# Modulation sums of an encoder layer: more of their terms on VectorE, one sum over partitions by matmul

## The chip, the cores and the metric

The kernel runs on one core of a Trainium2 chip. The metric is the device time of one execution in microseconds; the time before is the median of three runs. The core has a TensorE (PE in the profile; PEld is its weight load), a VectorE (DVE), a ScalarE (ACT), a GpSimd (POOL) and a SyncE (SP), which issues most of the plain loads. Each engine works its own list of instructions in order; the engines meet through semaphores.

## The reference

One layer of a streaming encoder on 1024 tokens of width 1024, in float32. Six vectors of 1024 numbers, made from one conditioning vector, shift, scale and gate the layer:

```python
cond = jax.nn.silu(c)
for l in range(DEPTH):                                   # DEPTH = 1
    mod = (cond @ w_mod[l] + b_mod[l])[:, None, :]       # w_mod: 1024 x 6144
    sh1, sc1, gt1, sh2, sc2, gt2 = jnp.split(mod, N_MOD, axis=-1)
    h = rms_norm(x, g_mix[l]) * (1.0 + sc1) + sh1
    p = h @ w_in[l]
    ...                                                  # HGRN2, S5 and RG-LRU on column groups of p
    x = x + gt1 * (y @ w_out[l])
    h2 = rms_norm(x, g_ffn[l]) * (1.0 + sc2) + sh2
    x = x + gt2 * peer_ffn(h2, peer_w_q[l], peer_sub_keys[l], peer_u[l], peer_v[l])
return rms_norm(x, g_final)
```

`peer_ffn` scores 8 heads against two sets of 128 keys, takes the 16 best of 16384 experts per token and head, and sums the gated rows of two tables of 16384 x 1024. The change concerns `cond @ w_mod` alone: a sum over 1024 inputs, that is over 8 blocks of 128 (KT = 8), for 48 blocks of 128 columns.

## The kernel before

Tokens are worked in four fronts F0 to F3 of 256 tokens (two tiles of 128). A front (`front`, L345) normalizes its tiles (`norm_x` L326, `norm_T` with the transposes at L337 and their eviction at L340), projects them with w_in (TensorE, `bank<-hT,w`), runs the S5 and LRU scans (L402, L447 and others on VectorE), the HGRN levels (masks, products and matmuls in turn: L540, L558 to L562 on VectorE, `wq<-q,kk` on TensorE), and projects out (gt1 enters at L621, the residual at L622). Then come the product keys (`product_keys`, L642: scores `wq<-hT,w` and `wq<-skT,qT` on TensorE, top-16 searches at L684 to L688 and sorting at L733 to L736 on VectorE). Tiles 0, 1, 6 and 7 get their experts by gathered rows (POOL's indirect loads at L921 and L937, row sums at L927 and L942 on VectorE), which run from F1 on beside the fronts; tiles 2 to 5 get theirs from the dense phase, the last half of the span, in which TensorE goes through all experts in 128 groups (transposes at L842 first), fed by one-hot gates (L790 to L797).

The modulation is made in twelve groups of 512 columns by `mod_rows(a, nv)` (L192). A group loads its part of w_mod in four loads of 512 KB (`load_w2`, L187 to L189, issued by SP in order). They come from the pool `w` with WPB = 3 buffers, shared with w_in, w_q and w_out, so that a load can start only when the third load before it has been used up. Each load holds two of the eight terms. A term is summed in one of two ways: as a matmul with cond's column, broadcast over 128 columns, as the weight (L201, in the profile L139 of the helper `mm`), which adds the 128 inputs and leaves the result in all partitions; or on VectorE as w times cond's column, added to a running sum `sv` in SBUF (L204 for the first, L206 for the others). In the second case one matmul with the constant `ones` at the end (L208) adds the 128 partitions of `sv` into the same PSUM bank. `nv` is the number of terms of the second kind, `MV = (2, 0)` (L55): two for the first norm's groups (a = 0, 4, 8, 12; column-wise by `mod_cols`), none for the others.

The other eight groups lie in two places. `late_mod` (L293) makes gt1 (a = 16, 20, `bc_row`) and four groups for the second norm (a = 24 to 36, `mod_cols`); it is stepped by the HGRN levels of F0. `bc_row("gt2", 40)` (L985) makes the last two groups, a = 40 and 44, after F1's product keys; `bc_row` adds b_mod at L289.

The order on each engine is not that of the program text. A list scheduler simulates the engines and puts each instruction where its inputs and its place in the program let it come next; so the order of before and that of after differ beyond the changed lines.

Of the kernel before, what the change touches and what calls it, by code (L numbers as in the profile page):

```python
# [21 lines left out]
KT = DM // 128  # L22
# [29 lines left out]
UHB = 3  # L52
UB = 3
WPB = 3
MV = (2, 0)  # L55
GT2 = 1
PORD = 1
PSTEP = 2
# [29 lines left out]
def trunk(ctx, tc, x, c, w_mod, b_mod, g_mix, w_in, hgrn_lb_logits, s5_a_re, s5_a_im, s5_b_re, s5_b_im,  # L88
# [31 lines left out]
    def bank():  # L120
        return ps.tile([128, 512], F32, name="bank")
# [4 lines left out]
    def T2():  # L126
        return t2.tile([128, 512], F32, name="t2")
# [10 lines left out]
    def mm(o, l, r, st, sp):  # L138
        P_.matmul(o, l, r, start=st, stop=sp)  # L139
# [4 lines left out]
    ones = const.tile([128, 128], F32, name="ones")  # L144
# [42 lines left out]
    def load_w2(w, k0, c0):  # L187
        t = wp.tile([128, 2, 512], F32, name="w")
        D.dma_start(out=t, in_=w[k0 * 128:(k0 + 2) * 128, c0:c0 + 512].rearrange("(k p) n -> p k n", p=128))  # L189
        return t  # L190

    def mod_rows(a, nv):  # L192

        pm = bank()
        sv = None
        for k0 in range(0, KT, 2):
            w = load_w2(w_mod, k0, a * 128)
            for k in range(2):
                ck = cond[:, k0 + k:k0 + k + 1]
                if k0 + k < KT - nv:  # L200
                    mm(pm, ck.to_broadcast([128, 128]), w[:, k], k0 + k == 0, k0 + k == KT - 1)  # L201
                elif sv is None:
                    sv = T2()
                    V.tensor_scalar(sv, w[:, k], ck, None, op0=OP.mult)  # L204
                else:
                    V.scalar_tensor_tensor(sv, w[:, k], ck, sv, op0=OP.mult, op1=OP.add)  # L206
        if nv:
            mm(pm, ones, sv, False, True)  # L208
        return pm

    def mod_cols(a):
        pm = mod_rows(a, MV[0] if a < 16 else MV[1])
        for i in range(4):
            jk = TS()[:, 0:128]
            V.scalar_tensor_tensor(jk, pm[:, i * 128:i * 128 + 128], 1.0, ident, op0=OP.mult, op1=OP.mult,
                                   accum_out=mod[:, a + i:a + i + 1])
        V.tensor_tensor(mod[:, a:a + 4], mod[:, a:a + 4], cv("b_mod", a, 4), OP.add)
# [64 lines left out]
    def bc_row(nm, a):  # L282
        t = (keep if nm == "gt2" else const).tile([128, DM], F32, name=nm)
        for half in range(2):
            hs = slice(half * 512, half * 512 + 512)
            c0 = a * 128 + half * 512
            br = T2()
            D.dma_start(out=br, in_=b_mod[:, c0:c0 + 512].to_broadcast([128, 512]))
            V.tensor_tensor(t[:, hs], mod_rows(a + 4 * half, MV[1]), br, OP.add)  # L289
            yield  # L290
        bcast[nm] = t
# [1022 lines left out]
```

## Time and profile before

| | us |
|---|---|
| median of 3 runs | 3209.16 (3196.37 to 3212.6) |
| the profiled execution | 3212.96 |
| its span in the trace | 3211.1 |
| TensorE busy | 2838.5 (88%) |
| VectorE busy | 2663.5 (83%) |
| GpSimd busy | 1322.7 (41%) |

The span is what the profiler saw from the first instruction to the last; 1.86 us of the execution lie outside. A busy share over the whole span is a mean over stages that differ; the table of stretches among the rows below tells them apart. [...] A float32 matmul appears as two MATMUL instructions.

### The profile page before, as it was taken

The page shows a single profiled execution, that of the slowest core. Times are in us where ns is not written, and L with a number is a line of the kernel's source. Part 1 is how long each engine was busy: PE and PEld are TensorE (multiplying, and loading weights), DVE is VectorE, ACT ScalarE, POOL GpSimd, SP SyncE. Part 2 cuts the span into 40 slices and gives each one's busy share as a digit, 9 for nine tenths or more (in the row PEclk, how much of TensorE's full clock was granted, in tenths as well). Part 3 has the DMA queues.
Part 4 walks back from the last instruction along what each step waited for, and adds up shares of the span by engine and source line. Part 5 has one row for each costly group of instructions (what it writes and reads, how often), then busy time and mean ns, then how long its engine had stood idle before and what let it go on. Part 6 is the DMA issues. An engine that isn't in the chain of part 4 may idle for free.

```text
span 3211.1 us, 45551 instructions
## 1 busy us (share of the span) xinstructions
PE 2838.5 (88%) x16525; PEld 2424.6 (76%) x16525; DVE 2663.5 (83%) x5540; ACT 1043.6 (32%) x1993; POOL 1322.7 (41%) x1155
## 2 busy tenths in 40 slices
PE   5998976789788985779599999999999999999996
PEld 3765865476676865658588889889888998988896
DVE  6241798689987999879899989999989999899955
ACT  3312321133166560466622222222222222222222
POOL 0000156534454335541054545555655555355501
PEclk8998986799779995789699999999999999999998
DMA  5353597899689986886499999999999999999932
GB/s 156 110 164 125 169 309 237 311 349 314 209 286 345 302 293 219 284 322 228 145 325 339 349 328 346 344 342 344 348 341 323 343 345 347 313 333 335 351 118 77
DMA packets 490370, 896.73 MB, mean 279 GB/s; under 512 B 29609, under 2 KB 306721, under 8 KB 486049
## 3 DMA queue, kind: packets, MB, share of 16 engines
q0 software_dynamic: 147456, 536.94, 46.6%
q1 hardware_dynamic: 333312, 342.92, 32.8%
q10 hardware_dynamic: 9376, 13.96, 1.2%
q8 instruction: 131, 2.15, 0.3%
q14 instruction: 95, 0.77, 0.1%
HBM read 847.57 MB, written 46.14 MB: 278 GB/s over the span
## 4 chain that ended last, share of the span: by engine, by line
PE 14%; issue 12%; DMA 9%; POOL 8%; DVE 6%; ACT 1%; SPq 0%; POOLq 0%; ACTq 0%; DVEq 0%
PE A L139 7%; PE V L139 6%; DMA row<-in_peer_v_dram,eid 5%; POOL row L921 4%; POOL row L937 4%; DMA row<-in_peer_u_dram,eid 2%; DMA vn<-in_peer_v_dram 2%; DVE fin L942 2%; DVE row L927 1%; PE T L842 1%; DVE vl L869 1%; DVE acc L882 1%; DVE ul L844 1%; DVE ag L854 0%; DMA row<-x1d 0%
## 5 line engine op out<-in xcount | busy, mean ns | idle before, releaser
L937 POOL DMA_INDIRECT row<-in_peer_v_dram,eid x512 | 631.6, 1234 | 672.8 <-DVE fin L942 362.2
L921 POOL DMA_INDIRECT row<-in_peer_u_dram,eid x512 | 644.6, 1259 | 610.3 <-DVE row L927 308.0
L139 PE MATMUL V<-vh,w 128*128 128x256 f32 x4096 | 771.0, 283 | 8.6 <-ACT w L856 4.9
L942 DVE SCALAR_TENSOR_TENSOR fin<-row,wgt,fin 128x1024 f32<-128x1024 f32 x508 | 649.1, 1278 | 50.9 <-DMA row<-in_peer_v_dram,eid 48.6
L927 DVE SCALAR_TENSOR_TENSOR row<-row,h 128x1024 f32<-128x1024 f32 x512 | 619.3, 1219 | 85.5 <-DMA row<-in_peer_u_dram,eid 84.1
L139 PEld LDWEIGHTS V<-vh,w 128*128 128x128 f32 x4096 | 645.5, 189 | 19.3 <-ACT w L856 8.2
L139 PE MATMUL V<-vl,w 128*128 128x256 f32 x2048 | 563.1, 282 | 7.1 <-DVE vl L869 7.1
L139 PE MATMUL A<-hh,ul 128*128 128x512 f32 x1024 | 408.6, 399 | 19.6 <-DVE ul L844 19.4
L139 PE MATMUL A<-hh,uh 128*128 128x512 f32 x1024 | 414.0, 404 | 0.4 <-ACT uh L843 0.3
L139 PE MATMUL A<-hl,uh 128*128 128x512 f32 x1024 | 404.4, 395 | 0.0
L139 PEld LDWEIGHTS V<-vl,w 128*128 128x128 f32 x2048 | 388.3, 190 | 13.0 <-DVE vl L869 9.7
L867 ACT CAST vh<-vn 128x1024 fp32r<-128x1024 f32 x128 | 134.6, 1052 | 447.5 <-PE V L139 370.9
L139 PE MATMUL bank<-hT,w 128*128 128x256 f32 x1152 | 270.1, 392 | 9.9 <-DMA w<-in_w_in_dram 4.7
L139 PEld LDWEIGHTS bank<-hT,w 128*128 128x128 f32 x1152 | 222.3, 197 | 45.1 <-issue 6.3
L139 PE MATMUL wq<-hT,w 128*128 128x256 f32 x1024 | 239.6, 388 | 7.4 <-DMA w<-in_peer_w_q_dram 5.6
L139 PEld LDWEIGHTS A<-hh,ul 128*128 128x128 f32 x1024 | 194.1, 190 | 61.8 <-DVE ul L844 28.3
L139 PE MATMUL gk<-oh 128*128 128x128 f32 x1024 | 177.0, 328 | 62.0 <-ACT oh L794 45.6
L843 ACT CAST uh<-T 128x512 fp32r<-128x512 f32 x256 | 147.4, 586 | 258.7 <-PE T L842 250.1
L139 PEld LDWEIGHTS gk<-oh 128*128 128x128 f32 x1024 | 161.8, 229 | 82.0 <-ACT oh L794 55.0
L139 PEld LDWEIGHTS A<-hl,uh 128*128 128x128 f32 x1024 | 194.0, 189 | 36.5
L139 PEld LDWEIGHTS A<-hh,uh 128*128 128x128 f32 x1024 | 194.2, 190 | 34.6 <-ACT uh L843 1.1
L139 PEld LDWEIGHTS wq<-hT,w 128*128 128x128 f32 x1024 | 194.8, 196 | 33.7 <-issue 5.9
(419 smaller groups left out, 3999.8 us busy)
## 6 DMA issues: line engine op xcount, KB each, us to landing
vn<-in_peer_v_dram SPq DMA_DIRECT2D x128, 512.0 KB
un<-in_peer_u_dram SPq DMA_DIRECT2D x128, 512.0 KB
w<-in_w_in_dram SPq DMA_DIRECT2D x88, 512.0 KB
w<-in_peer_w_q_dram SPq DMA_DIRECT2D x64, 512.0 KB
gd<-stg SPq DMA_DIRECT2D x32, 1024.0 KB
gt<-gd SPq DMA_DIRECT2D x16, 2048.0 KB
w<-in_w_mod_dram SPq DMA_DIRECT2D x48, 512.0 KB
w<-in_w_out_dram SPq DMA_DIRECT2D x32, 512.0 KB
```

Of the source, the lines that this page charges most:

```text
L139: P_.matmul(o, l, r, start=st, stop=sp)
L842: P_.transpose(bk[:, k], un[:, kk * 128:kk * 128 + 128], ident)
L843: S.copy(uh, bk)
L844: V.tensor_tensor(ul, bk, uh.bitcast(F32), OP.subtract)
L867: S.copy(vh, vn)
L869: V.tensor_tensor(vl, vn, vh.bitcast(F32), OP.subtract)
L882: V.tensor_tensor(a, a, pv, OP.add)
L921: G.indirect_dma_start(out=ur, out_offset=None, in_=u_tab, in_offset=bass.IndirectOffsetOnAxis(ap=o.eid[:, k:k + 1], axis=0))
L927: V.scalar_tensor_tensor(ur, ur, 1.0, o.h2, op0=OP.mult, op1=OP.mult, accum_out=o.act[:, k:k + 1])
L937: G.indirect_dma_start(out=vr, out_offset=None, in_=v_tab, in_offset=bass.IndirectOffsetOnAxis(ap=o.eid[:, k:k + 1], axis=0))
L942: V.scalar_tensor_tensor(o.fin, vr, o.wgt[:, k:k + 1], o.fin, op0=OP.mult, op1=OP.add)
```

## The change

The first norm's groups now have four terms of eight on VectorE instead of two, and the eight other groups have all eight there instead of none. Where all eight are there, the ones-matmul is the only matmul of its group, and it starts the bank as well as closing it.

```diff
@@ -52,7 +52,7 @@
 UHB = 3
 UB = 3
 WPB = 3
-MV = (2, 0)
+MV = (4, 8)
 GT2 = 1
 PORD = 1
 PSTEP = 2
@@ -198,14 +198,14 @@
             for k in range(2):
                 ck = cond[:, k0 + k:k0 + k + 1]
                 if k0 + k < KT - nv:
-                    mm(pm, ck.to_broadcast([128, 128]), w[:, k], k0 + k == 0, k0 + k == KT - 1)
+                    mm(pm, ck.to_broadcast([128, 128]), w[:, k], k0 + k == 0, False)
                 elif sv is None:
                     sv = T2()
                     V.tensor_scalar(sv, w[:, k], ck, None, op0=OP.mult)
                 else:
                     V.scalar_tensor_tensor(sv, w[:, k], ck, sv, op0=OP.mult, op1=OP.add)
         if nv:
-            mm(pm, ones, sv, False, True)
+            mm(pm, ones, sv, nv == KT, True)
         return pm
 
     def mod_cols(a):
```

The scheduler's order moves with it. Three places are shown; in each row the line comes first, then the operation, the result and the inputs with their names, the shape, and how many such instructions stand in a row. On TensorE at gt2's place (`bank<-w,cond` are gt2's terms, `wq` F1's product keys, L337 the transposes of F2's normalized tiles `s_`, `bank<-hT,w` F2's projections), this stands before:

```order
L139 MATMUL wq<-skT,qT 128x128 x2
L139 MATMUL bank<-w,cond 128x512 x2
L139 MATMUL wq<-skT,qT 128x128 x2
L139 MATMUL bank<-w,cond 128x512 x8
L337 MATMUL bank<-ident,s_4649 128x128 x4
L139 MATMUL bank<-w,cond 128x512 x2
L337 MATMUL bank<-ident,s_4649 128x128 x4
L139 MATMUL bank<-w,cond 128x512 x2
L337 MATMUL bank<-ident,s_4677 128x128 x4
L139 MATMUL bank<-w,cond 128x512 x2
L337 MATMUL bank<-ident,s_4677 128x128 x4
L139 MATMUL bank<-hT,w 128x256 x72
```

Here gt2's matmuls and the transposes take turns. After the change, with `t_4623` and `t_4645` the two running sums that come from VectorE, the same place reads:

```order
L139 MATMUL wq<-skT,qT 128x128 x2
L139 MATMUL wq<-hT,w 128x256 x8
L139 MATMUL wq<-skT,qT 128x128 x4
L139 MATMUL bank<-t_4623,ones 128x512
L139 MATMUL bank<-t_4645,ones 128x512
L337 MATMUL bank<-ident,s_4665 128x128 x8
L337 MATMUL bank<-ident,s_4693 128x128 x8
L139 MATMUL bank<-hT,w 128x256 x72
```

F2's transposes stood among the last matmuls of gt2; now both ones-matmuls stand ahead of all of them.

On VectorE at the same place (L684 to L736 are F1's product keys, L942 the row sums of a gathered tile, L289 the addition of b_mod), this stands before:

```order
L942 SCALAR_TENSOR_TENSOR fin<-row,wgt,fin 128x1024
L733 TENSOR_TENSOR oh<-io_727,pf 128x800
L686 MATCH_REPLACE rest_4334<-vals,sc 128x128
L686 MATCH_REPLACE rest_4340<-vals,sc 128x128
L942 SCALAR_TENSOR_TENSOR fin<-row,wgt,fin 128x1024
L735 TENSOR_TENSOR oh<-oh,cidx 128x800
L719 CAST pf<-pos 128x64
L687 MAX vals<-rest_4334 128x8
L687 MAX vals<-rest_4340 128x8
L289 TENSOR_TENSOR gt_4605<-bank,t_4626 128x512
```

Here gt2 appears only as the addition at L289. After the change:

```order
L206 SCALAR_TENSOR_TENSOR t_4645<-w,cond,t_4645 128x512
L733 TENSOR_TENSOR oh<-io_727,pf 128x800
L942 SCALAR_TENSOR_TENSOR fin<-row,wgt,fin 128x1024
L688 MAX_INDEX inds<-vals,rest_4433 128x8
L704 TENSOR_TENSOR cand<-vals 128x4x16
L688 MAX_INDEX inds<-vals,rest_4439 128x8
L206 SCALAR_TENSOR_TENSOR t_4645<-w,cond,t_4645 128x512
L735 TENSOR_TENSOR oh<-oh,cidx 128x800
L942 SCALAR_TENSOR_TENSOR fin<-row,wgt,fin 128x1024
L695 CAST fi<-inds 128x128
L684 MAX best<-cand 128x8 x4
L736 TENSOR_REDUCE ef<-oh 128x2x8
```

The sixteen terms stand one by one between other operations, and the last of them stands just ahead of an L735 of F1's sorting. On VectorE in F0's HGRN levels (`q`, `kk` and `scT` are the levels' operands, `mod` the late columns), this stands before:

```order
L437 TENSOR_TENSOR u<-u,ys 128x512
L540 COPY_PREDICATED scT<-masks,wq 128x32x8 x2
L561 TENSOR_TENSOR q<-q,pr_1301 128x64x8
L562 TENSOR_TENSOR kk__759<-kk__759,pr_1301 128x64x8
L540 COPY_PREDICATED scT<-masks,wq 128x16x16 x2
L561 TENSOR_TENSOR q<-q,pr_1343 128x32x16
L562 TENSOR_TENSOR kk__759<-kk__759,pr_1343 128x32x16
L215 SCALAR_TENSOR_TENSOR s_1322,mod<-bank,ident 128x128
L215 SCALAR_TENSOR_TENSOR s_1324,mod<-bank,ident 128x128
L215 SCALAR_TENSOR_TENSOR s_1326,mod<-bank,ident 128x128
```

One level follows the other here. After the change:

```order
L540 COPY_PREDICATED scT<-masks,wq 128x32x8 x2
L561 TENSOR_TENSOR q<-q,pr_1309 128x64x8
L562 TENSOR_TENSOR kk__759<-kk__759,pr_1309 128x64x8
L289 TENSOR_TENSOR gt_1070<-bank,t_1116 128x512
L204 TENSOR_SCALAR t_1184<-w,cond 128x512
L206 SCALAR_TENSOR_TENSOR t_1184<-w,cond,t_1184 128x512 x7
L204 TENSOR_SCALAR t_1263<-w,cond 128x512
L206 SCALAR_TENSOR_TENSOR t_1263<-w,cond,t_1263 128x512 x7
L215 SCALAR_TENSOR_TENSOR s_1200,mod<-bank,ident 128x128
L215 SCALAR_TENSOR_TENSOR s_1202,mod<-bank,ident 128x128
L215 SCALAR_TENSOR_TENSOR s_1204,mod<-bank,ident 128x128
L204 TENSOR_SCALAR t_1316<-w,cond 128x512
```

Between two levels now stand the terms of two whole groups, one after the other.

## Rows read from the trace of the kernel before

**Rows 1.** The page's busy times, shares of the span and instructions of each engine.

```profile
PE 2838.5 (88%) x16525; PEld 2424.6 (76%) x16525; DVE 2663.5 (83%) x5540; ACT 1043.6 (32%) x1993; POOL 1322.7 (41%) x1155
```

**Rows 2.** Busy time by stretch of the span (start:end, length, engines, clock, DMA).

```profile
core 0: us, PE busy (x) PEld busy (x) DVE busy (x) ACT busy (x) POOL busy (x), PEclk, DMA share, GB/s
...
155.20:228.40 73.20, 71.80 (x375) 45.45 (x375) 34.34 (x88) 5.87 (x8) 0.00 (x0) 1.00 0.61 186
466.00:520.00 54.00, 31.82 (x190) 31.03 (x190) 52.66 (x93) 1.88 (x2) 32.64 (x23) 0.50 0.68 218
690.00:740.00 50.00, 45.43 (x202) 35.07 (x201) 50.00 (x249) 8.55 (x21) 17.71 (x28) 0.97 0.96 317
...
800.00:840.00 40.00, 29.38 (x169) 20.84 (x162) 40.00 (x86) 3.42 (x5) 15.46 (x14) 0.85 0.78 250
...
900.00:1040.00 140.00, 116.76 (x562) 93.98 (x563) 110.09 (x125) 91.22 (x219) 68.88 (x51) 0.87 0.93 331
1040.00:1220.00 180.00, 158.36 (x883) 134.97 (x881) 175.98 (x583) 95.99 (x213) 62.11 (x64) 0.93 0.87 292
...
1440.00:1600.00 160.00, 119.57 (x615) 105.73 (x614) 150.23 (x577) 105.75 (x248) 13.48 (x31) 0.81 0.54 187
1600.00:3200.00 1600.00, 1557.40 (x10227) 1403.15 (x10225) 1413.42 (x1882) 431.93 (x676) 797.04 (x642) 0.99 0.89 316
```

**Rows 3.** One term on each engine: nanoseconds (shortest/median/longest), first and last start.

```profile
L139 PE MATMUL bank<-w,cond x176: 592/592/1221, 12.9 to 747.2; 128*128 128x512 f32 x176
L204 DVE TENSOR_SCALAR t<-w,cond x4: 481/486/487, 22.7 to 51.4; 128x512 f32<-128x512 f32 x4
L206 DVE SCALAR_TENSOR_TENSOR t<-w,cond,t x4: 744/748/752, 23.8 to 52.0; 128x512 f32<-128x512 f32 x4
```

**Rows 4.** Instructions with cond alone, by place: PE, PEld, DVE, ACT.

```profile
12.00:54.00 42.00, 28.23 (x48) 10.92 (x48) 4.93 (x8) 0.21 (x1) 0.92 0.64 192
160.00:226.00 66.00, 44.29 (x96) 17.14 (x96) 0.00 (x0) 0.00 (x0) 1.00 0.62 190
724.00:750.00 26.00, 16.82 (x32) 6.18 (x32) 0.00 (x0) 0.00 (x0) 0.93 0.94 313
```

**Rows 5.** SP's timeline: start, length of the issuing, line, load, how many.

```profile
0.75 46.75 SPq L189 DMA_DIRECT2D w<-in_w_mod_dram  x16
...
151.37 67.05 SPq L189 DMA_DIRECT2D w<-in_w_mod_dram  x24
...
716.96 22.61 SPq L189 DMA_DIRECT2D w<-in_w_mod_dram  x8
741.48 50.08 SPq L184 DMA_DIRECT2D w<-in_w_in_dram  x14
```

**Rows 6.** TensorE's timeline at gt2 and the start of F2's projections.

```profile
732.06 7.11 PE L139 MATMUL bank<-w,cond 128*128 128x512 f32 x12 [3.00 <-DMA w<-in_w_mod_dram]
...
745.83 1.98 PE L139 MATMUL bank<-w,cond 128*128 128x512 f32 x4 [0.94 <-DMA w<-in_w_mod_dram]
...
749.84 17.53 PE L139 MATMUL bank<-hT,w 128*128 128x256 f32 x80 [1.59 <-ACT hT L340]
```

**Rows 7.** TensorE's timeline in F0: the last transposes and the first projection.

```profile
67.44 1.97 PE L337 MATMUL bank<-ident,s 128*128 128x128 f32 x8 [6.83 <-ACT s L329]
...
72.37 3.92 PE L139 MATMUL bank<-hT,w 128*128 128x256 f32 x15
```

**Rows 8.** VectorE's timeline: the L735 ahead of which the last term now stands.

```profile
775.37 0.98 DVE L735 TENSOR_TENSOR oh<-oh,cidx 128x800 f32<-128x800 f32 x1
```

**Rows 9.** TensorE's waits from 760 to 850: total, times, longest.

```profile
PE wq L139 <- DVE q L545: 6.8, 1, 6.8
PE wq L139 <- DVE kk__4705 L562: 6.2, 1, 6.2
PE wq L139 <- DVE kk__4705 L559: 3.8, 1, 3.8
```

## The prediction

> **What bounds the kernel now.** I read the shares of the engines first, then the same shares stage by stage, and then the two stages that the change touches, on the engines' own timelines. Over the whole span TensorE is busy 88% and VectorE 83% [rows 1], which decides nothing: the two take turns as the bound. The table by stretch shows it [rows 2]. From about 1600 us to the end (the dense experts) TensorE is busy 1557.40 of 1600 us, and nothing that the change touches lies there, so this stage moves as a block: what counts is when it starts. Ahead of it are the four fronts F0 to F3 and their routing. In 155.2 to 228.4, where F0's late modulation runs among the HGRN levels, TensorE has 71.80 of 73.20 us and VectorE only 34.34. From F1's end on it is the other way round: VectorE has 50.00 of 50 us in 690 to 740, 40.00 of 40 in 800 to 840, 175.98 of 180 in 1040 to 1220 and 150.23 of 160 in 1440 to 1600. Only 900 to 1040 leaves it much room, 110.09 of 140. So the change takes work from TensorE where TensorE is full, which is fair (the late modulation), and also where VectorE is full already (gt2, 717 to 750 us).
>
> The third thing to see is the pace of the weight loads. SP issues 16 loads for the first norm in 46.75 us, 24 for the late modulation in 67.05 us and 8 for gt2 in 22.61 us [rows 5]: 2.8 to 2.9 us for each load of two terms, three times the same. Two terms cost TensorE about 2.4 us (four instructions at 592 ns) and VectorE 1.5 us (two at 748 ns) [rows 3]. The loads, not the engine that takes them in, set the pace, so a cheaper consumer wins little by itself.
>
> **First norm's columns.** Two more of eight terms go to VectorE in each of four groups: 8 matmuls (16 of the 48 TensorE instructions there, 28.23 us in all [rows 4], so 9.4 us) against 8 VectorE operations of 748 ns [rows 3], 6.0 us. Both lie in a stretch paced by 16 loads. At best the end of the stage comes earlier by what the last group saves: its last two loads are drained by VectorE beside TensorE, and the ones-matmul comes after. Ends: 0 if the loads set it alone, and -6 if two thirds of the 9.4 us were on the path. I take -2, since the pace of 2.9 us is the same with and without VectorE's help.
>
> **Late modulation (six groups in F0).** Removed are 48 matmuls, 96 instructions and 44.29 us of TensorE [rows 4]; 6 ones-matmuls of two instructions return, 12 at 592 ns = 7.1 us. Added to VectorE are 6 groups of 0.486 + 7 x 0.748 = 5.72 us [rows 3], 34.3 us, on top of 34.34: 68.7 us of work in a stage that lasted 73.20 [rows 2]. The floor by VectorE is 68.7, by loads 67.05; so the most that can be won is 5. But VectorE's list is in order, and it holds two whole groups in a row between HGRN levels: 8 loads, at 2.8 us 22.4 us, against 11.4 us of terms, so VectorE stands some 11 us for loads there, with the levels' masks and products queued behind it, and TensorE waiting for those. 68.7 + 11 = 79.7, or +6. Ends: -5 (terms slip into gaps) and +16 (a second such wait). Most like the row of F1's levels (466 to 520), where VectorE has 52.66 of 54 us and TensorE gets no further for it. I take +6. With the first norm, +4.
>
> **gt2, the term that decides.** 16 matmuls, 32 instructions and 16.82 us of TensorE [rows 4] go; two ones-matmuls return. VectorE gets 2 x 5.72 = 11.4 us where it has no idle time [rows 2]. In the kernel before the last of these matmuls run at 732 to 747 us between F2's transposes, and F2's projections start at 749.84 [rows 6]. In the changed order both ones-matmuls stand ahead of F2's transposes on TensorE, and the sixteenth term stands on VectorE directly ahead of the L735 that started at 775.37 [rows 8]: the scheduler has spread the terms, one between every few steps of F1's product keys and row sums. TensorE, being in order, cannot begin F2 before that. Counting VectorE's list with the trace's durations, 8.3 of the 11.4 us stand ahead of that point net (3.1 us of other work moved behind it), so the last term ends near 783.7. Then a ones-matmul (1.1), the transposes and evictions: one tile took 4.93 us from the first transpose to its projection [rows 7], the second adds about 3. F2's projections start near 793, **+43** against 749.84. The w_in loads behind gt2's eight loads in SP's queue now wait for buffers that VectorE frees; the first w_in load needs only the buffer of the sixth load, so it lands well ahead of 793 and costs nothing beyond the +43 (if a row said otherwise, one load, 2.8).
>
> **What comes back.** While F2 is held, VectorE doesn't idle: the order moves some 42 us of other work (row sums and F1's routing) ahead of F2's first LRU operation. That work is then missing later, which shortens only stretches in which VectorE is the bound. In F2's own levels TensorE waited 6.8 + 6.2 + 3.8 = 16.8 us for VectorE [rows 9]; about 10 of it should go, as the routing that crowded VectorE is done. In 1040 to 1220 and 1440 to 1600, which are full [rows 2], the list is some 8 and 15 us shorter than before; I take half, 12. In 900 to 1040 VectorE has slack and nothing returns. The ends are 10 (only the levels) and 42 (all). I take 22, the middle, since the full and the slack stretches about share the time.
>
> Sum: 4 + 43 - 22 = **+25**. The profiled execution took 3212.96 us, 3211.1 of it the span; 3238. The median of the runs is 0.12% lower, so 3234.
>
> [...]
>
> **Rivals.** (1) The forecast: F2 is held behind VectorE's terms and about half comes back. For it speaks that both queues are in order and that VectorE is full there; 0.52. Its own range, from the ends above, is 3213 to 3256.
>
> (2) VectorE is the bound all the way from F1 to the dense phase: the whole 42 us comes back, and only the early +4 and a small rest, 5 to 13 us, remain: about 3218. For it speak the full stretches [rows 2]; against it the 30 us that VectorE idles in 900 to 1040, in which F2's chain and not VectorE's amount of work sets the end. 0.23.
>
> (3) Faster. The place is F2's stretch behind its projections, and the mechanism that VectorE's crowding was F2's real limit: then F2, started late, runs with an emptied VectorE and saves the 42 us of moved work and also the whole 16.8 us of its waits, while the early stages reach their floors (-2 and -5). 43 - 59 - 7 = -23, 3186 by the median. It decides from the point where more than 50 us are recovered. Against it: the moved row sums only lie on F2's chain where they stood between its operations, and F2's levels waited 16.8 us in all, not 50. 0.11.
>
> (4) Nothing comes back. TensorE, sparse in the late modulation and idle for some 45 us ahead of F2, falls to the lower clock, as in 466 to 520 [rows 2]; F2's first projections (17.53 us at full clock [rows 6]) take up to twice that, which eats the recovery, and the late stage is at its upper end, +16: -2 + 16 + 43 = +57, 3266 by the median. 0.14.
>
> That the change does nothing of the kind is out: TensorE's list holds 16 matmuls with the condition vector where it held 88.
>
> **How the numbers follow.** The time is that of (1), 3234. The range is 3206 to 3262: below it lies (3), above it half of (4) and a small tail of (1). About 0.5%, 16 us, is what a measurement of this kernel can tell from no change, so faster means below 3193 and slower above 3225. Faster: most of (3), 0.08. Same: (2), the rest of (3) and the lower part of (1), 0.31. Slower: the rest of (1) and (4), 0.61.
>
> **What would show it.** On TensorE's timeline of the changed kernel, F2's first projection near 793 (right), or near 750 (wrong: the hold isn't there). A gap on TensorE from about 728 to 784, ended by VectorE's sums. The late stage 74 to 84 us long instead of 73.2; under 70, and TensorE's relief was worth more than I gave it. The first matmuls of the dense phase some 25 us later than before: 45 or more speaks for (4), under 13 for (2), earlier for (3). In 900 to 1040 VectorE should still idle; if its idle time there is gone, (2) has taken the place of (1). The prediction is wrong in its main step if VectorE's last gt2 term ends before 765, because the terms did not have to wait for the work that stands ahead of them.

## The result and the profile after

The changed kernel takes 3242.11 us in the median of 6 runs (3231.94 to 3249.19), against 3210.55 us (3196.37 to 3213.58) for the kernel before: a ratio of 1.0111, interval 1.0092 to 1.0129. It is slower by some 32 to 36 us, and the interval lies clear of 1; 3234 with a range of 3206 to 3262 was forecast. The profiled execution took 3241.63 us with a span of 3239.8.

The busy times of the whole span, which answer to [rows 1], show that the work moved as planned and tell nothing of the loss: TensorE has 16397 instructions, 128 fewer, and is busy 2800.2 us, 38 less; VectorE has 5612, 72 more, and is busy 2712.2 us, 49 more.

Where it went is seen by following the same points of the program through both traces. The times are starts in us: the first projection of F0 and F2 on TensorE, the G projection at the end of F0's levels, the last residual (L622) of F2 and F3 and the first LRU operation (L447) of F3 on VectorE, the first transpose of the dense phase on TensorE.

| | before | after | later by |
|---|---|---|---|
| F0, first projection | 72.37 | 68.28 | -4.1 |
| F0, G projection | 244.64 | 245.78 | +1.1 |
| F2, first projection | 749.84 | 792.63 | **+42.8** |
| F2, last residual | 1006.3 | 1055.3 | +48.9 |
| F3, first LRU operation | 1119.1 | 1170.7 | +51.6 |
| F3, last residual | 1409.7 | 1443.6 | +33.9 |
| dense phase | 1595.88 | 1628.25 | +32.4 |
| end of the span | 3211.1 | 3239.8 | +28.7 |

Each start here and below comes from one profiled execution, and such starts scatter. In the nine kernels of this document that leave the first norm as it was, F0's first projection begins anywhere from 70.1 to 74.7. So a difference of 2 or 3 us says nothing, and one of 30 or 40 stands.

The step is at F2's start. TensorE's timeline there, which answers to [rows 6] (start, length, line, operation; in brackets the idle time before it and what ended it):

```profile
726.24 0.71 PE L139 MATMUL wq<-skT,qT 128*128 128x128 f32 x4 [0.84 <-ACT qT L656]
754.57 2.08 PE L139 MATMUL bank<-t,ones 128*128 128x512 f32 x2 [27.61 <-DVE t L206]
784.81 2.07 PE L139 MATMUL bank<-t,ones 128*128 128x512 f32 x2 [28.17 <-DVE t L206]
786.67 1.06 PE L337 MATMUL bank<-ident,s 128*128 128x128 f32 x4
...
792.63 13.44 PE L139 MATMUL bank<-hT,w 128*128 128x256 f32 x48 [0.53 <-ACT hT L340]
```

TensorE does nothing from 727 to 785 but the two ones-matmuls, each of which waits some 28 us for VectorE's running sum. F2's transposes stand behind the second. VectorE's timeline says when the sum was done; the second row is the L735 of [rows 8]:

```profile
784.02 0.73 DVE L206 SCALAR_TENSOR_TENSOR t<-w,cond,t 128x512 f32<-128x512 f32 x1
784.67 0.98 DVE L735 TENSOR_TENSOR oh<-oh,cidx 128x800 f32<-128x800 f32 x1
```

And the stretches of the table [rows 2], after the change (PEclk is the granted TensorE clock as a share of full speed, the number behind x the count of instructions). VectorE was full in 740 to 800 while TensorE had 14.33 of 60 us, at a granted clock of 0.54:

```profile
740.00:800.00 60.00, 14.33 (x41) 9.24 (x42) 60.00 (x180) 6.56 (x18) 21.58 (x25) 0.54 0.71 220
800.00:840.00 40.00, 37.40 (x163) 31.46 (x162) 37.26 (x80) 13.32 (x25) 22.30 (x21) 0.96 0.99 326
...
900.00:1040.00 140.00, 113.32 (x659) 96.03 (x659) 118.21 (x134) 76.69 (x176) 75.52 (x51) 0.84 0.79 273
```

SP's queue at the same place, which answers to [rows 5]: gt2's loads now take 37.72 us for seven and one more at 765.48, where eight took 22.61, since a load waits for a buffer that VectorE's terms free (715 to 770: five of the eight loads waited for VectorE, at L206 and L686 to L688, 37.3 us in all, and the other three for TensorE's `wq`, 10.6 us); F2's w_in loads come 30 us later.

```profile
717.19 37.72 SPq L189 DMA_DIRECT2D w<-in_w_mod_dram  x7
...
765.48 0.37 SPq L189 DMA_DIRECT2D w<-in_w_mod_dram  x1
771.56 69.44 SPq L184 DMA_DIRECT2D w<-in_w_in_dram  x14
```

### The profile page after: what moved, and what is told of

The parts are those of the page before. It is cut to its first block, busy times and chain, and to the rows that moved or that the text cites. A ratio compares the mean times of both kernels' runs of the same rounds, so it can differ in the third digit from the quotient of the medians.

```text
span 3239.8 us, 45359 instructions
## 1 busy us (share of the span) xinstructions
PE 2800.2 (86%) x16397; PEld 2413.9 (75%) x16397; DVE 2712.2 (84%) x5612; ACT 1044.8 (32%) x1995; POOL 1343.6 (41%) x1155
## 4 chain that ended last, share of the span: by engine, by line
PE 39%; DVE 23%; DMA 16%; issue 11%; POOL 6%; ACT 5%; ACTq 0%; SPq 0%; POOLq 0%; DVEq 0%
PE A L139 12%; PE V L139 11%; PE bank L139 7%; DVE row L927 6%; DMA row<-in_peer_u_dram,eid 5%; DMA row<-in_peer_v_dram,eid 5%; PE wq L139 4%; POOL row L937 3%; DVE fin L942 3%; POOL row L921 3%; PE gk L139 2%; PE T L842 2%; DMA vn<-in_peer_v_dram 1%; DMA w<-in_w_mod_dram 1%; DVE oh L790 1%
## 5 line engine op out<-in xcount | busy, mean ns | idle before, releaser
L937 POOL DMA_INDIRECT row<-in_peer_v_dram,eid x512 | 649.9, 1269 | 647.6 <-DVE fin L942 343.3
L942 DVE SCALAR_TENSOR_TENSOR fin<-row,wgt,fin 128x1024 f32<-128x1024 f32 x508 | 649.3, 1278 | 42.0 <-DMA row<-in_peer_v_dram,eid 39.3
L139 PE MATMUL A<-hh,ul 128*128 128x512 f32 x1024 | 407.8, 398 | 21.1 <-DVE ul L844 21.1
L139 PE MATMUL bank<-hT,w 128*128 128x256 f32 x1152 | 272.5, 394 | 16.4 <-DMA w<-in_w_in_dram 8.1
L139 PEld LDWEIGHTS A<-hh,uh 128*128 128x128 f32 x1024 | 193.9, 189 | 34.3 <-ACT uh L843 1.1
L139 PE MATMUL gk<-oh 128*128 128x128 f32 x1024 | 173.9, 325 | 48.5 <-ACT oh L794 38.1
```

The source lines that it names most:

```text
L937: G.indirect_dma_start(out=vr, out_offset=None, in_=v_tab, in_offset=bass.IndirectOffsetOnAxis(ap=o.eid[:, k:k + 1], axis=0))
L942: V.scalar_tensor_tensor(o.fin, vr, o.wgt[:, k:k + 1], o.fin, op0=OP.mult, op1=OP.add)
```

## The experiments

Theory H: the loss is F2's late start behind gt2's sums. Rival W: VectorE is the bound, and each us of work that it gets costs time wherever it lies. Rival L: the late groups in F0 disturb what follows. The profile's line numbers are those of the kernel before or differ from them by a few where lines were added or taken out. Ratios are against the kernel before on the same chip, with 95% intervals.

**e1 to e4: which part of the change.** A third number in `MV` gives gt2 its own count; the four kernels differ in it alone (in the cut below the notes behind # are added).

```diff
-MV = (4, 8)
+MV = (4, 0, 0)     # e1: first norm only
+MV = (2, 8, 0)     # e2: late groups only
+MV = (2, 0, 8)     # e3: gt2 only
+MV = (4, 8, 0)     # e4: all but gt2
...
-            V.tensor_tensor(t[:, hs], mod_rows(a + 4 * half, MV[1]), br, OP.add)
+            V.tensor_tensor(t[:, hs], mod_rows(a + 4 * half, MV[2] if nm == "gt2" else MV[1]), br, OP.add)
```

e1: 

> Only the first norm's columns are changed: four terms of eight on VectorE, the eight other groups as before. Theory H (the loss is F2's wait behind gt2's ones-matmul): 3207 us, -3 to -4 against the kernel before, as the first projection in F0 comes 4 us earlier and nothing else moves. Rival W (VectorE is the bound, each us of work added there costs the same share, 31.6 us of loss for 51.8 us of work, 0.61): 6.0 us added, 3214.

Measured: 1.0011 (0.999 to 1.0032), no difference. F0's first LRU operation came 4.0 us early, F0's last residual 2.2. That nothing else moves did not hold: in this trace F2's first projection came 8.1 us early and the dense phase 6.5, and the time gained nothing by it.

e2: 

> Only the six late groups in F0 have all terms on VectorE; first norm as before, gt2 by matmuls as before. H: +5, 3215 or less (the late stage took 5 us longer in the changed kernel and F0 ended 1 us late). W: 34.3 us of work added, +21, 3231. Rival L (the late groups disturb the order of all that follows): +25 or more, 3235.

Measured: 1.0012 (0.9992 to 1.0031), no difference; F0's end 2.5 us late. 34.3 us of VectorE work more and 44 us of term matmuls less on TensorE in F0 come to nothing either way. L falls, and W with it for this place.

e3: 

> Only gt2's two groups have all terms on VectorE. H: the whole loss, +28 to +33, 3241; F2's projections start near 790. W: 11.4 us added, +7, 3217. L: 3211.

Measured: 1.0131 (1.0107 to 1.0155), 3250.76 us: gt2 alone loses 42 us, as much as the whole change or more. F2's projections start at 798.33.

e4: 

> The changed kernel with gt2's two groups back on TensorE. H: 3212, +1, F2's projections near 750. W: 40.4 us of work added, +24, 3235. L: +25 or more.

Measured: 0.9949 (0.992 to 0.9978), 3196.99 us against 3206.66: with gt2 back on TensorE the rest of the change is a gain of 0.5% (6 runs; about the least that can be told). F2's projections start at 750.01. W falls again: 40.3 us of added VectorE work, and the kernel is faster. Of the gain itself nothing is seen up to F3's last residual (-0.0 us in its trace); the dense phase starts 7.3 us and the span ends 15.4 us earlier. Since e1 and e2 alone gain nothing, it is not the sum of the two, and which wait it came from stays open.

**e5 and e12: the ones-matmuls moved behind F2's front.** The terms stay where they are; the sums lie in gt2's own tile `t`, and the ones-matmuls and the additions stand in the program behind F2's front. e5 is the changed kernel so edited, e12 the kernel before with gt2 alone so done. The last argument of `mod_rows` says what it does: 1 makes the terms alone, 2 the ones-matmul alone.

```diff
         drain(side)
+        if b == GT2 + 1:
+            for half in range(2):
...
+                V.tensor_tensor(gt2t[0][:, hs], mod_rows(40 + 4 * half, KT, gt2t[0][:, hs], 2), br, OP.add)
+            bcast["gt2"] = gt2t[0]
...
         if b == GT2:
-            for _ in bc_row("gt2", 40):
-                pass
+            gt2t.append(keep.tile([128, DM], F32, name="gt2"))
+            for half in range(2):
+                mod_rows(40 + 4 * half, KT, gt2t[0][:, half * 512:half * 512 + 512], 1)
```

e5: 

> The changed kernel, but gt2's two ones-matmuls and the additions of b_mod stand in the program behind F2's front; the running sums lie in gt2's own tile meanwhile. VectorE's work is that of the changed kernel, and TensorE has nothing of gt2 ahead of F2's transposes. H: F2's projections start at 735 to 760, and the loss is gone: 3200 to 3215. W: 51.8 us of work added as in the changed kernel, 3242.

Measured: 1.009 (1.0064 to 1.0115). The loss is not gone, so H as I had put it fails here. TensorE's first F2 projection, SP's queue and what SP waited for in e5 (total us, times, longest) say what had taken the place:

```profile
760.94 6.30 PE L139 MATMUL bank<-hT,w 128*128 128x256 f32 x16 [36.63 <-DMA w<-in_w_in_dram]
```

```profile
715.32 40.01 SPq L189 DMA_DIRECT2D w<-in_w_mod_dram  x8
756.15 49.31 SPq L184 DMA_DIRECT2D w<-in_w_in_dram  x14
```

```profile
SPq L189 <- DVE gt L205: 20.3, 3, 7.8
```

F2's transposes are done before 699.7, but its weights are not there. gt2's eight loads hold the three buffers until VectorE, with no idle time from 715 to 743, has taken their terms (L205 here is L206 of the other kernels); the w_in loads stand behind them in SP's queue. So there are two chains from VectorE's terms to F2's start, one over the ones-matmul and one over the buffers, and the shorter is 11 us late by itself. What e5 costs in all is not explained by that: F2 starts 31.7 us earlier than in the changed kernel, and the ratio falls only from 1.0111 to 1.009. In its trace e5 loses another 13.7 us between F2's last residual (7.9 us late) and F3's first LRU operation (21.6 us late), and no run shows why.

e12: 

> As e5 (gt2's terms on VectorE, its ones-matmuls behind F2's front), but with the first norm and the late groups as before, so that gt2 alone differs from the kernel before. F2's projections should start 8 to 15 us late again, because w_in's loads wait behind gt2's loads for buffers that VectorE's terms free. If F2's start alone counts, at the 0.65 us for each us of e6: +5 to +10, 3211 to 3216. If something else of the terms' place (the loads held between F1 and F2) costs besides, as e5's +0.9% suggests: +20 or more, 3226.

Measured: 1.0054 (1.0035 to 1.0073), +17 us; F2's first projection at 763.99 (+14.2), again after a wait of 35.00 us for w_in; the dense phase 14 us late. The effect is gt2's own, and it is between the two numbers expected: here about one us for each us of F2's start.

**e6: a late F2 without any terms.** The kernel before, with F2's scale made to depend on F1's sorting.

```diff
-            norm_T(xn, hT, j, gmod, mod[:, 0:8])
+            norm_T(xn, hT, j, gm2[0] if t0 == 4 else gmod, mod[:, 0:8])
...
                     route_part(vals[j], inds[j], E_, rs[j], h0)
+                    if t0 == 2 and h0 == 0 and j == 1:
+                        gm2.append(const.tile([128, KT], F32, name="gmod2"))
+                        V.scalar_tensor_tensor(gm2[0], rs[j][1][:, 2, 8:16], 0.0, gmod, op0=OP.mult, op1=OP.add)
```

> The kernel before, with one small VectorE operation more (128x8): F2's scale is copied through it and made to depend on the sixth L736 of F1's sorting, the one behind which gt2's last term stood in the changed kernel. So F2's transposed tiles are evicted only after that, and VectorE has 0.1 us of work more. H: F2's projections start 25 to 40 us late, and the time is 3225 to 3245. W: 3211.

Measured: 1.0069 (1.0048 to 1.009), 22 us by the ratio. TensorE's timeline shows the hold that was built:

```profile
778.82 1.12 PE L337 MATMUL bank<-ident,s 128*128 128x128 f32 x4 [29.12 <-ACT hT L340]
...
781.61 13.06 PE L139 MATMUL bank<-hT,w 128*128 128x256 f32 x48 [0.28 <-ACT hT L340]
```

A late start alone, with 0.1 us of work added, goes with a loss of 22 us, some two thirds of that of the changed kernel. It gives back more than the changed kernel does: 31.8 us at F2's start, 15.9 at the dense phase.

**e9: the work without the wait.** Sixteen operations like gt2's terms, meant for their place, on data that is there already, with a result that nothing reads; TensorE's list is that of the kernel before.

```diff
...
+            for k in range(8 if nm == "gt2" else 0):
+                V.scalar_tensor_tensor(jw[0], bcast["gt1"][:, hs], efs[0][:, 0, k:k + 1], bcast["gt1"][:, hs],
+                                       op0=OP.mult, op1=OP.add)
             V.tensor_tensor(t[:, hs], mod_rows(a + 4 * half, MV[1]), br, OP.add)
```

> The kernel before, with sixteen VectorE operations of 128x512 more, whose result nothing uses, of the kind and at the place of gt2's terms in the changed kernel (they stand one by one among F1's product keys, TensorE's list is that of the kernel before). Theory H+W (the loss at gt2 is about 0.6 us for each us that F2 starts late, and VectorE's work there costs its full 12 us besides): 3213 to 3218, +8 to +12. Rival H (only F2's start counts): 3206 to 3209, 0 to +3.

Measured: 0.999 (0.9975 to 1.0005). All 16 ran, 11.8 us in all (grouped by line for 700 to 820: busy us, mean ns, idle before), one by one among F1's product keys, in a stretch in which VectorE had no idle time. They started at 739.6 to 796.6, some 12 us later than gt2's terms in the changed kernel (727.6 to 784.0), and F2's projections, which had no cause to wait for them, started at 753.67, ahead of the last twelve:

```profile
L292 DVE SCALAR_TENSOR_TENSOR jw<-gt,ef 128x512 f32<-128x512 f32 x16 | 11.8, 740 | 0.0
```

```profile
740.00:800.00 60.00, 55.30 (x242) 44.97 (x242) 60.00 (x150) 26.76 (x51) 18.76 (x16) 0.97 0.88 281
```

W falls here too: the 7 us that it asks for 11.8 us of work lie outside the interval. Work on a full engine cost nothing in this stretch. What it pushed back, against the kernel before, were the row sums of 750 to 900 (by 8 to 24 us) and F1's searches and sorting, while the products of F2's HGRN levels (L561, L562 of the kernel before) stand within 2 us of where they stood. That nobody waited soon for what was pushed back is argued from these starts. The same work with F2 waiting for it costs 42 us (e3).

**e7, e10 and e11: gt2 moved behind F2's start.** gt2's groups are issued among F2's levels, as the late groups are in F0's: by matmul with the rest as before (e7), with all terms on VectorE (e10), and by matmul with the first norm and the late groups as in the changed kernel (e11).

```diff
         if b == 0:
             side.append(late_mod())
+        if b == GT2 + 1:
+            side.append(bc_row("gt2", 40))
...
-        if b == GT2:
-            for _ in bc_row("gt2", 40):
-                pass
```

e7: 

> The kernel before, with gt2's groups (by matmul, as before) issued among F2's HGRN levels instead of ahead of F2, as the late groups are in F0's. H: if F2's start is what counts, taking the 16.8 us of gt2's matmuls and its eight loads away from it brings F2's projections forward to 730 to 745 and saves 3 to 12 us: 3198 to 3207. W: no change in VectorE's work, 3210.

Measured: 0.9973 (0.9945 to 1.0), F2's projections at 733.44, 16 us early, and the dense phase 14.4 us early. As expected, at the edge of what can be told.

e10: 

> The kernel of e7 (gt2 issued among F2's levels, first norm and late groups as before) with all eight terms of gt2's groups on VectorE, so that sixteen terms lie in F2 and none ahead of it. H+W: F2 starts 10 to 15 us early as in e7, and the 11.4 us of work come on top of e7's time: 3207 to 3212. H: the time of e7, 3199.

Measured: 0.9991 (0.9975 to 1.0008), no difference from the kernel before, where the same terms in front of F2 cost 42 us (F2's projections start at 728.79, the ones-matmuls run at 836.92 and 874.02, and TensorE stands 5.8 us in all for their sums). Whether they cost something against e7 is not settled: 0.18% more, 6 us, lies between the 0 of H and the 11 of H+W, and the intervals of the two runs overlap.

e11: 

> The kernel of e4 (first norm four terms, late groups eight terms on VectorE, gt2 by matmul) with gt2's matmuls among F2's levels as in e7. If the gains of e4 (-0.5%) and of e7 (-0.3%) add: 3181, -24. If both came from the same place (the order behind F2): 3195, -10.

Measured: 0.9993 (0.9978 to 1.0007): both expectations missed. Its trace is the earliest of all up to the dense phase (1578.27, -17.6 us) and gives it all back there. (The profiled execution took 3213.42 us, the median of e11's 12 runs is 3203.08, so part of what the trace shows is this execution's own; but the median too is that of the kernel before.) The dense phase of the kernel before, and that of e11:

```profile
1595.90:3211.00 1615.10, 1561.50 (x10240) 1406.29 (x10240) 1418.93 (x1897) 436.57 (x681) 797.04 (x642) 0.99 0.89 315
```

```profile
1578.30:3211.60 1633.30, 1566.31 (x10240) 1408.12 (x10240) 1431.57 (x1918) 435.79 (x682) 791.72 (x642) 0.98 0.89 311
```

The same 10240 matmul instructions, 18 us longer; TensorE waited 30.8 us for VectorE's `ul` (L844) where it waited 19.4 before. VectorE has 21 operations and 13 us more in that phase. So the dense phase is no block of fixed length, and what is won ahead of it is not all kept.

**e8: half of gt2's terms.** `MV = (2, 0, 4)`.

> gt2's groups with four terms on VectorE and four on TensorE, all else as before. In the order the first ones-matmul stands ahead of F2's transposes and the second among the projections. H: the wait is set by where the fourth term of each group stands, roughly half: +5 to +18, 3215 to 3228. W: 5.9 us of work added, +4, 3214.

Measured: 1.0058 (1.0034 to 1.0081), +19 us; F2's projections at 767.20 (+17.4), the dense phase 14.0 us late. The upper end of H; W's +4 (1.0012) is out.

Set side by side, by F2's first projection, the start of the dense phase (both in us against the kernel before, one profiled execution each) and the ratio:

| | F2 | dense phase | ratio |
|---|---|---|---|
| e10, terms in F2 | -21.1 | -10.6 | 0.9991 |
| e7, gt2 by matmul in F2 | -16.4 | -14.4 | 0.9973 |
| e1, first norm only | -8.1 | -6.5 | 1.0011 |
| e4, all but gt2 | +0.2 | -7.3 | 0.9949 |
| e2, late groups only | +2.0 | -5.7 | 1.0012 |
| e9, work alone | +3.8 | +3.2 | 0.999 |
| e5, ones late, changed kernel | +11.1 | +19.5 | 1.009 |
| e12, ones late, gt2 only | +14.2 | +14.1 | 1.0054 |
| e8, gt2 half | +17.4 | +14.0 | 1.0058 |
| e6, hold alone | +31.8 | +15.9 | 1.0069 |
| changed kernel | +42.8 | +32.4 | 1.0111 |
| e3, gt2 only | +48.5 | +43.5 | 1.0131 |

F2 starts late in every one of the slower kernels and in none of the others, and e6 and e9 tell the late start from the work. How much a late start costs is not shown: e6 gets half back by the dense phase and e12 nothing, and e5 loses 0.9% with F2 only 11.1 us late. Each kernel has its own order from the scheduler, and e4, whose F2 is on time, shows that the rest of an order can move the time by 0.5%. So the losses of e6, e8 and e12, 0.5 to 0.7%, agree with the late start without proving its price; those of e3 and the changed kernel are too large for that.

## Why the prediction was right, step by step

**What bounds where.** Right: the loss is where VectorE was full and something on TensorE stood behind it, and the place where TensorE had been full (the late groups) gave and cost nothing measurable by itself (e2).

**First norm, -2 forecast.** -4.1 at F0's first projection, inside the ends of 0 and -6. The five kernels with four terms there begin it at 65.0 to 68.3, the nine with two at 70.1 to 74.7, so the gain is real.

**Late groups, +6 forecast.** From F0's first projection to its G projection it took 172.27 us before and 177.50 after, +5.2, but that is no measure of the late groups alone: in e1, which leaves them as they were, it took 176.0. The levels by themselves, from the first product (`wq<-q,kk`) to the first output (`bank<-scT,v`), took 66.31 us before and 69.45 after, +3.1; they took 65.7 to 66.3 in all nine kernels without late terms on VectorE and 68.7 to 71.2 in the five with them. VectorE did wait for loads between the levels, though not for the 11 us at the two whole groups: there it waited 0.62, 0.94, 0.42 and 0.89 us,

```profile
194.71 1.54 DVE L206 SCALAR_TENSOR_TENSOR t<-w,cond,t 128x512 f32<-128x512 f32 x2 [0.62 <-DMA w<-in_w_mod_dram]
197.18 0.49 DVE L204 TENSOR_SCALAR t<-w,cond 128x512 f32<-128x512 f32 x1 [0.94 <-DMA w<-in_w_mod_dram]
...
200.56 1.54 DVE L206 SCALAR_TENSOR_TENSOR t<-w,cond,t 128x512 f32<-128x512 f32 x2 [0.42 <-DMA w<-in_w_mod_dram]
202.98 1.54 DVE L206 SCALAR_TENSOR_TENSOR t<-w,cond,t 128x512 f32<-128x512 f32 x2 [0.89 <-DMA w<-in_w_mod_dram]
```

since SP issued the last 17 of the 24 loads in 39.61 us, 2.3 us each. The forecast reckoned with 2.8, and said that the loads and not the engine that takes them in set that pace. That reading was wrong. In the kernel before, SP spent most of the 67.05 us of these 24 loads waiting for TensorE to free a buffer (150 to 225: total, times, longest):

```profile
SPq L189 <- PE bank L139: 60.3, 24, 6.0
```

The term has the right sign, half the size, and a reason that holds in small part. The stage was then some 76 us long (73.20 + 3.1), as the sign of 74 to 84 had it. For the sum of the two, +4 was forecast and +1.1 came, which can't be told from nothing: F0's G projection starts at 242.7 to 248.0 in the eight kernels with neither change and at 241.1 to 245.8 in the four with both.

**gt2's hold, +43 forecast.** Right, with its reason: the last term ended at 784.75 (783.7 forecast), directly ahead of the L735, and F2's projections began at 792.63 (793 forecast, +42.8). That it is right to the microsecond is luck: two errors of 1 us cancel, and in e3 the same edit in another order gives +48.5.

**The loads behind gt2's in SP's queue, 0 forecast.** In the changed kernel that held: at F2's start TensorE waits for the sum, not for w_in. But the prediction put it at nothing, under cover of the other, and e5 and e12 show that it is a second chain of 11 to 14 us on its own as soon as the ones-matmul is out of the way.

**What comes back, 22 forecast.** This is the term that was mis-sized: 42.8 at F2's start is 32.4 at the dense phase, 10.4 back, the lower end of 10 to 42. The forecast was 10 in F2's own levels and 12 in the full stretches behind them. The step that failed is F2's levels: TensorE still waits 14.4 + 3.3 us for VectorE there (after, 760 to 960: total, times, longest), against the 16.8 of [rows 9], and F2's last residual is 48.9 late, 6 more than its start.

```profile
PE wq L139 <- DVE kk__4721 L562: 14.4, 3, 9.4
PE wq L139 <- DVE q L545: 3.3, 1, 3.3
```

Up to F3's first LRU operation the delay grows by 8.8. What comes back, 17.7, comes in F3, from 51.6 late at its first LRU operation to 33.9 at its last residual, and next to nothing (1.5) between that and the dense phase. Half of it comes between F3's G projection (1310.4 before, 42.7 late) and its last residual (1409.7), a stretch that the prediction left out: it says that only 900 to 1040 leaves VectorE much room, but in the kernel before VectorE is also idle for 24 us of 1340 to 1440.

```profile
1340.00:1440.00 100.00, 79.87 (x351) 58.71 (x351) 75.59 (x116) 62.81 (x149) 49.17 (x36) 0.80 0.87 312
```

The prediction argued with the amount of VectorE's work that was moved ahead (42 us). e9 shows for the stretch at gt2 that the amount of work on VectorE need not be what a front waits for; what F3 made up its 17.7 us by stays open.

**Sum.** +25 was forecast, and +28.7 came in the span. The terms 4 + 43 - 22 measured 1.1 + 41.7 - 10.4 = 32.4 at the dense phase, which then ran 3.7 us shorter. The prediction had moved that phase as a block; its length differs from trace to trace by more than that (e11).

**The rivals.** The sign for them was the dense phase: 25 us late for (1), under 13 for (2), 45 or more for (4); it is 32.4 late. (2), all comes back: out, and in 900 to 1040, as was said against it, VectorE still idles (118.21 busy of 140 us). (3), faster: out. (4), nothing comes back: out at its +57; what came back is about half way between its nothing and the forecast's 22, but neither of its reasons came at the size it needs. The late stage was not at its upper end of +16. The clock did fall, to 0.54 in 740 to 800, where TensorE had 14.33 of 60 us (1.00 before, with 54.99 us), and to 0.63 in 155.2 to 228.4, where it had 54.34 of 73.20 us (1.00 before, with 71.80). But F2's first 48 projection instructions took 13.44 us at a clock of 0.79 and the next 48 took 12.29 at 0.86, where at the 17.53 us for 80 of [rows 6], at 1.00, 48 would have taken 10.5: by this estimate the clock cost some 5 us, not the 17.5 of that rival. The 48 behind those had 1.00 again and took 10.73.

## What to carry to other kernels

Ask of moved work who stands behind its result, not how full the engine is that gets it: sixteen operations on a full VectorE cost nothing where no matmul stood behind them (e9), and 42 us where two matmuls, and behind them a whole stage, waited in another engine's list (e3). Such work has two results, the value and the free buffer; moving the reader of the value away is not enough while the loads of the next stage wait for the buffer in the same queue (e5, e12). What a late start lost came back by half in one order (e6) and not at all in another (e12): take the lower end for what a late stage makes up.

The fastest version measured is e4, the change without gt2: 0.9949 of the time before (0.992 to 0.9978). Its gain has no wait to its name, and e11, which has the same terms on VectorE and gt2 moved, does not have it (0.9993); so it is a gain of this one order, not yet a rule.

## What was not expected of the hardware

The dense phase, in which TensorE is busy 97% of the time, was between 1602.5 us (e9: 1599.04 to 3201.5) and 1633.3 us (e11) long with the same matmuls, in one profiled execution of each kernel. A granted clock of 0.54 for 60 us, a stretch with 14.33 us of TensorE work, cost some 5 us in the matmuls behind it by the estimate above: it was 0.79 in the first 48 projection instructions and 0.86 in the next, and 1.00 in 820.86 to 840, from 28 us after the first of them (48 in 10.73 us).
